# A token-major mixer residual, modulation sums over a feature-major weight copy, and rope tables from the start of the program

## The chip, the cores and the metric

The kernel runs on one core of a Trainium2 chip. The metric is the device time of one execution in microseconds (us); lower is better. The engines are TensorE (PE, its weight loads as PEld), VectorE (DVE), ScalarE (ACT), GpSimd (POOL) and SyncE (SP), whose queue here only issues DMAs.

## The reference

One decoder block over 256 tokens of width 2048, in float32: six modulation vectors from a conditioning vector, a mixer of gated linear attention (GLA) and latent attention (MLA) with a merged output, a SwiGLU FFN and a last RMSNorm. Cut to what matters here:

```python
ang = positions.astype(jnp.float32)[..., None] * inv_freq      # rope, 32 frequencies
cos, sin = jnp.cos(ang), jnp.sin(ang)
mod = (silu(c) @ ada_w + ada_b).reshape(B, 6, D)
shift_m, scale_m, gate_m, shift_f, scale_f, gate_f = mod       # m = 0 .. 5
h = rmsnorm(x, norm_mix_g) * (1 + scale_m) + shift_m
x = x + gate_m * token_mix(h, cos, sin, w_in, ..., w_out)      # ends with merged @ w_out
h = rmsnorm(x, norm_ffn_g) * (1 + scale_f) + shift_f
x = x + gate_f * swiglu(h, ffn_w_in, ffn_w_down)
return rmsnorm(x, final_norm_g)
```

## The kernel before

All weights (408 MB with the modulation weights) come once from memory. A weight tile, 128 partitions x 1024 elements of float32 (512 KB, "a half"), is loaded by SP (`load_raw`, L98), split by an ACT cast into a high part `hi` (L107) and by VectorE into the rest `lo` (L108), and used in three matmuls per tile: hi x hi, lo x hi, hi x lo. `form_a` (L166 to L168) holds the activations still and streams 512 weight columns, and gives token-major results; `form_b` (L176 to L178) holds the weights and streams 256 tokens, and gives feature-major ones (features on the partitions). So a form_b step has twice the matmuls of half the columns.

The stages in order: a start that loads x, turns it feature-major and modulates the first two of 16 feature blocks; the input projection in four rounds r = 0 to 3 over growing parts of the features, so that it can begin before all of the modulation is there; attention of both kinds; the output projections mla_wo and gla_wo; w_out; the FFN's two halves; the final norm.

The modulation is background work. `ada_steps(m, c0)` loads 512 columns of `ada_w` in eight loads; each is scaled by silu(c) and added up on VectorE (L265, L267), two passes of 128x512 per load. The sum over the 128 partitions is then made by four TensorE transposes (L289) whose copies on ACT add up (L291). m = 0, 1 are used by `modulate` (L320 to L322), which makes the FFN's or mixer's input from normed x; m = 2 is the mixer's gate, m = 3, 4 are the FFN's, m = 5 the FFN's gate, which has a POOL all-reduce (L300) in place of the transposes. `pace` sets how many background steps go beside each half; `background(n)` does n steps at once. In `w_out` `background(1000)` ahead of column 3 clears what is left. Where `hold` is set, or with `keep_in_program_order`, an instruction keeps its place in its engine's row; the others are placed by a scheduler when the program is built, and each engine then goes through its row in order.

Load buffers go round: six `raw` tiles, and four more cut from a free slot (`more_raw`; slot 5 in the output projections), so ten there. A load waits until its buffer has been read.

w_out is done in four columns i = 0 to 3 of 512 features by `form_b`. Its results are multiplied by the gate and added to x in feature-major form (L846); x comes back from a copy in DRAM, `x_sp`, written in round 3 (L428, L843). Sums of squares for the FFN's norm are made by ACT and TensorE (L853 to L858), then `rsqrt_mean` (L193 to L206), `rows_of` (L212, L213) and 16 `modulate`. In the FFN `turn_x1` (L899) turns the residual token-major again for the end.

The rope angles (`rope_angles`, L351 to L374) are 40 POOL operations over 128 x 256 angles, in rounds 1 and later; the tables are made in round 3.

Of the kernel before, what the change touches and what calls it, by code (L numbers as in the profile page):

```python
# [17 lines left out]
D = 2048  # L18
# [16 lines left out]
def _consts():  # L35
    j = np.arange(P)
    f = np.zeros((P, 256 + 2), np.float32)
# [3 lines left out]
    f[:, 256] = inv[j % 32]  # L41
    f[:, 257] = np.where(j < 64, 1.0, -1.0)
# [9 lines left out]
def tile_block(ctx: ExitStack, tc: tile.TileContext, x, positions, ada_w, ada_b, w_in, gla_gk_w, gla_wo,  # L52
# [138 lines left out]
    def rsqrt_mean(dst, ssq, n, w, eng=None):  # L191
# [3 lines left out]
        V.tensor_scalar(out=yi, in0=v.bitcast(I32), scalar1=1, scalar2=None, op0=ALU.logical_shift_right)  # L195
        V.tensor_scalar(out=yi, in0=yi, scalar1=-1.0, scalar2=float(0x5F3759DF), op0=ALU.mult, op1=ALU.add)
# [25 lines left out]
    cft = const.tile([P, 258], F32, name="cft")  # L222
# [5 lines left out]
    nc.gpsimd.dma_start(out=cft, in_=cf)  # L228
# [14 lines left out]
    def ada_steps(m, c0, cols=512, quick=None):  # L243
        kk = 1024 // cols
        accs = [sb(512, t, 2 if t == "ada" else 1)[:, :cols]
                for t in (("ada",) if quick is None else ("ada", "w2" if m else "w3"))]
        b0, nb = m * 16 + c0 // P, cols // P
        cs = slice(b0, b0 + nb)
        ps = None if quick is None else aux_bank()
        n = 0  # L250
        for k0 in range(0, KT, kk):
            raw = load_raw(ada_w[0, k0 * P:(k0 + kk) * P, m * D + c0:m * D + c0 + cols], kk, cols)

            def add(k0=k0, raw=raw):
# [758 lines left out]
```

## Time and profile before

| what | value |
|---|---|
| three runs, median | 1746.09 us (1744.71 to 1747.65) |
| profiled execution, device time | 1749.17 us |
| its span in the trace | 1747.1 us |
| mean granted TensorE clock | 0.987 |
| TensorE / VectorE / ACT / POOL busy | 98% / 70% / 49% / 6% |
| HBM read | 408.51 MB, 239 GB/s over the span |

The device time contains some 2 us outside the span. Terms are reckoned on the span and carried to the median. A matmul's busy time overlaps the next one's, so distances between starts, or a count over a full stretch, tell what one costs.

### The profile page before, as it was taken

What the parts mean: (1) busy time and instruction counts of PE and PEld (TensorE: products, weight loads), DVE (VectorE), ACT (ScalarE), POOL (GpSimd) and SP (SyncE); (2) the same over time, 40 slices, a digit from 0 to 9 for tenths busy, and PEclk for the clock granted to TensorE, in tenths of its full rate; (3) what the DMA queues carried; (4) which work ended last, traced back from release to release, by engine and by line L of the source; (5) the groups of instructions that cost most, each with busy time, mean ns of one, the idle gap of its engine ahead of it and who ended that gap; (6) DMA issues with size and microseconds to landing.
All of it is one profiled execution on the core that took longest, in us unless ns stands there. A gap on an engine that the chain in (4) does not pass through costs nothing. (4 is left out here: it accounts for less than half of the span.)

```text
span 1747.1 us, 24089 instructions
## 1 busy us (share of the span) xinstructions
PE 1705.2 (98%) x8888; PEld 1461.1 (84%) x8888; DVE 1226.6 (70%) x1764; ACT 847.6 (49%) x1300; POOL 99.7 (6%) x136
## 2 busy tenths in 40 slices
PE   6999999999999999999999899999999999999997
PEld 5898899889999887788899888888888888788885
DVE  6899987587787477988887856666664444555556
ACT  4644445355766655544444444444444444444443
POOL 1370000000000001000000000000000000000001
PEclk8999999999999999999999899999999999999998
DMA  9999897655455498999998678778776666555652
GB/s 353 323 325 314 300 302 226 182 188 170 144 151 180 123 313 259 343 372 349 336 323 297 212 206 272 242 232 277 240 232 191 182 191 190 178 189 191 192 191 99
DMA packets 207349, 418.47 MB, mean 240 GB/s; under 512 B 12960, under 2 KB 31840, under 8 KB 206592
## 3 DMA queue, kind: packets, MB, share of 16 engines
q1 hardware_dynamic: 205472, 410.39, 72.1%
q0 software_dynamic: 1616, 6.49, 1.0%
q8 instruction: 69, 1.13, 0.3%
q14 instruction: 48, 0.39, 0.1%
q10 hardware_dynamic: 144, 0.07, 0.0%
HBM read 408.51 MB, written 8.39 MB: 239 GB/s over the span
## 5 line engine op out<-in xcount | busy, mean ns | idle before, releaser
L108 DVE TENSOR_TENSOR lo<-raw,hi 128x1024 fp32r<-128x1024 f32 (+3 forms) x524 | 600.9, 1152 | 396.9 <-ACT hi L107 394.4
L107 ACT CAST hi<-raw 128x1024 fp32r<-128x1024 f32 (+3 forms) x524 | 512.4, 984 | 620.6 <-PE mm L168 391.1
L167 PE MATMUL mm<-lo,s 128*128 128x512 f32 (+1 forms) x1520 | 598.4, 394 | 2.6 <-DVE lo L108 2.6
L168 PE MATMUL mm<-hi,s 128*128 128x512 f32 (+1 forms) x1520 | 590.4, 390 | 1.7 <-DVE s L322 1.7
L166 PE MATMUL mm<-hi,s 128*128 128x512 f32 (+1 forms) x1520 | 543.2, 393 | 4.3 <-ACT hi L107 2.1
L166 PEld LDWEIGHTS mm<-hi,s 128*128 128x128 f32 x1520 | 286.7, 190 | 63.3 <-ACT s L321 3.1
L167 PEld LDWEIGHTS mm<-lo,s 128*128 128x128 f32 x1520 | 287.8, 189 | 61.4 <-DVE lo L108 5.2
L168 PEld LDWEIGHTS mm<-hi,s 128*128 128x128 f32 x1520 | 287.3, 189 | 58.7 <-DVE s L322 2.0
L267 DVE SCALAR_TENSOR_TENSOR ada<-raw,cact,ada 128x512 f32<-128x512 f32 (+1 forms) x293 | 211.1, 724 | 10.5 <-DMA raw<-in_ada_w_dram 7.6
L176 PE MATMUL mm<-s,hi 128*128 128x256 f32 x672 | 191.7, 286 | 0.0
L177 PE MATMUL mm<-s,hi 128*128 128x256 f32 x672 | 190.1, 284 | 0.0
L178 PE MATMUL mm<-s,lo 128*128 128x256 f32 x672 | 188.3, 284 | 0.0
L107 ACT CAST hi<-s 128x1024 fp32r<-128x1024 f32 (+1 forms) x76 | 78.2, 1029 | 106.5 <-PE mm L168 46.2
L176 PEld LDWEIGHTS mm<-s,hi 128*128 128x128 f32 x672 | 128.7, 192 | 0.8 <-issue 0.3
L177 PEld LDWEIGHTS mm<-s,hi 128*128 128x128 f32 x672 | 128.8, 192 | 0.4
L178 PEld LDWEIGHTS mm<-s,lo 128*128 128x128 f32 x672 | 127.5, 192 | 0.0
L108 DVE TENSOR_TENSOR lo<-s,hi 128x1024 fp32r<-128x1024 f32 (+1 forms) x76 | 91.7, 1207 | 27.1 <-ACT hi L107 26.5
L926 PE MATMUL mm<-lo,w 128*128 128x512 f32 x160 | 62.7, 392 | 0.0
L927 PE MATMUL mm<-hi,w 128*128 128x512 f32 x160 | 62.4, 392 | 0.0
L267 DVE SCALAR_TENSOR_TENSOR ada<-s,cact,ada 128x512 f32<-128x512 f32 (+1 forms) x79 | 57.7, 730 | 0.5
L925 PE MATMUL mm<-hi,w 128*128 128x512 f32 x160 | 50.5, 394 | 0.7 <-ACT w L933 0.7
L451 DVE TENSOR_TENSOR s<-mm,s 128x512 f32<-128x512 f32 (+1 forms) x62 | 40.1, 672 | 0.2
(270 smaller groups left out, 1594.1 us busy)
## 6 DMA issues: line engine op xcount, KB each, us to landing
raw<-in_ffn_w_in_dram SPq DMA_DIRECT2D x176, 512.0 KB, 4.4
raw<-in_ada_w_dram SPq DMA_DIRECT2D x150, 512.0 KB, 4.9
raw<-in_w_in_dram SPq DMA_DIRECT2D x128, 512.0 KB, 4.7
raw<-in_ffn_w_down_dram SPq DMA_DIRECT2D x88, 512.0 KB, 4.4
s<-in_ada_w_dram SPq DMA_DIRECT2D x42, 512.0 KB, 5.9
s<-in_w_in_dram SPq DMA_DIRECT2D x32, 512.0 KB, 4.7
raw<-in_mla_wo_dram SPq DMA_DIRECT2D x20, 512.0 KB, 6.5
raw<-in_gla_wo_dram SPq DMA_DIRECT2D x20, 512.0 KB, 6.9
```

Of the source, the lines that this page charges most:

```text
L107: A.copy(out=hh_, in_=rr)
L108: V.tensor_tensor(out=ll_, in0=rr, in1=hh_.bitcast(F32), op=ALU.subtract)
L166: T.matmul(ps[t][:, :cols], lhsT=ah[:, k, ts], rhs=hi, start=st, stop=False)
L167: T.matmul(ps[t][:, :cols], lhsT=ah[:, k, ts], rhs=lo, start=False, stop=False)
L168: T.matmul(ps[t][:, :cols], lhsT=al[:, k, ts], rhs=hi, start=False, stop=en)
L176: T.matmul(o, lhsT=hi[:, pick], rhs=ah[:, k], start=st, stop=False, skip_group_check=True)
L177: T.matmul(o, lhsT=hi[:, pick], rhs=al[:, k], start=False, stop=False, skip_group_check=True)
L178: T.matmul(o, lhsT=lo[:, pick], rhs=ah[:, k], start=False, stop=en, skip_group_check=True)
L267: ins = V.scalar_tensor_tensor(out=acc, in0=raw[:, k - k0], scalar=c, in1=acc, op0=ALU.mult, op1=ALU.add)
L925: T.matmul(o, lhsT=ah[:, ts], rhs=hi[:, ns], start=first, stop=False)
L926: T.matmul(o, lhsT=ah[:, ts], rhs=lo[:, ns], start=False, stop=False)
L927: T.matmul(o, lhsT=al[:, ts], rhs=hi[:, ns], start=False, stop=last)
```

## The change

1. m = 0, 1. A transposed copy `ada_t` of the first 4096 columns of `ada_w` is a new input. `ada_cols(k)` computes shift and scale of one block of 128 features: four loads of 128 features x 1024 inputs, each multiplied by a row copy `crow` of silu(c) and summed along the row by one VectorE `tensor_tensor_reduce` (L256). `modulate` of this block follows at once. `crow` is built at the start by four VectorE operations, four matmuls with ones (L414) and four ACT copies.
2. m = 2, 3, 4. The sum over partitions is a POOL `partition_all_reduce` (L294, 12 of them); for m = 3, 4 VectorE then takes the diagonal of four 128x128 blocks (L301), for m = 2 the row goes to DRAM `gm_sp` (L297) and comes back broadcast (L863). Each of these 12 groups has one `yield` more, a background step without a load. The four groups of m = 2 now come first.
3. w_out uses `form_a`; x1 is token-major, x is read again from the input (L866), gate and addition are two VectorE operations per token half (L888, L889), ACT squares with a sum. In column 3 the last two halves are kept, so that token half 0 is done first. Ahead of the FFN x1 is turned feature-major by 32 transposes (L905); `turn_x1` is gone.
4. The rope angles are 64 columns wide, made by POOL at the start; `rope_tables` (L384 to L395) copies and transposes them. Its call stands in round 3 of the program text, without pinning.
5. `rsqrt_mean` has one operation less, and at the start runs on VectorE. Small buffers are arranged anew; rounds 0 to 2 have nine load buffers, before eight.

```diff
+    def ada_cols(k, now=False):
+        for m in (1, 0):
+            c = m * 16 + k
+            part = sb(1, "md", 4)
+            for hf in range(2):
+                raw = raw_tile()
+                nc.sync.dma_start(out=raw, in_=ada_t[m * D + k * P:m * D + (k + 1) * P, hf * 1024:(hf + 1) * 1024])
+
+                def dot(raw=raw, hf=hf, c=c, part=part):
+                    V.tensor_tensor_reduce(out=raw, in0=raw, in1=crow[:, hf * 1024:(hf + 1) * 1024], scale=1.0,
+                                           scalar=part if hf else cb[:, c:c + 1], op0=ALU.mult, op1=ALU.add,
+                                           accum_out=mod[:, c:c + 1] if hf else part)
...
+        modulate(k, xTk, rx, 0, hhk, hlk)
...
-        elif m < 5:
-            ps = aux_bank()
-            for i in range(nb):
-                T.transpose(out=ps[:, i * P:(i + 1) * P], in_=acc[:, i * P:(i + 1) * P], identity=ident)
-            for i in range(nb):
-                A.activation(out=acc[:, i * P:(i + 1) * P], in_=ps[:, i * P:(i + 1) * P], func=AF.Copy,
-                             accum_out=mod[:, b0 + i:b0 + i + 1])
+        if m in (2, 3, 4):
+            ar = sb(512, "ada", 2)
+            G.partition_all_reduce(ar, acc, channels=P, reduce_op=bass_isa.ReduceOp.add)
+            yield
+            if m == 2:
+                tc.keep_in_program_order(nc.sync.dma_start(out=gm_sp[:, c0:c0 + cols], in_=ar[0:1]))
+                return
             for i in range(nb):
+                d = ar[:, i * P:(i + 1) * P]
+                V.tensor_tensor_reduce(out=d, in0=d, in1=ident, scale=1.0, scalar=0.0, op0=ALU.mult, op1=ALU.add,
+                                       accum_out=mod[:, b0 + i:b0 + i + 1])
...
+    def rope_tables(ang, ang2):
+        four = sb(512, "sc", 2)
+        V.scalar_tensor_tensor(out=ang2, in0=ang, scalar=-1.0, in1=ang, op0=ALU.mult, op1=ALU.max)
+        V.tensor_scalar(out=ang2, in0=ang2, scalar1=-1.0, scalar2=float(np.float32(np.pi / 2)), op0=ALU.mult,
+                        op1=ALU.add)
+        ps = aux_bank()
+        for i, a in enumerate((ang, ang2)):
+            A.copy(out=four[:, i * S:(i + 1) * S].rearrange("p (t r f) -> p t r f", t=2, r=4),
+                   in_=a.rearrange("p (t f) -> p t f", t=2).unsqueeze(2).broadcast_to([P, 2, 4, 32]))
+            for t in range(2):
+                c = slice(i * S + t * P, i * S + (t + 1) * P)
+                T.transpose(out=ps[:, c], in_=four[:, c], identity=ident)
+        A.activation(out=sin_t, in_=ps[:, 0:S], func=AF.Sin, scale=sgn)
+        A.activation(out=cos_t, in_=ps[:, S:2 * S], func=AF.Sin)
...
+    bg += [ada_steps(2, 512 * b) for b in range(4)]
     for b in range(4):
-        bg += [ada_steps(m, 512 * b) for m in (2, 4, 3)]
+        bg += [ada_steps(m, 512 * b) for m in (4, 3)]
...
     for i in range(4):
         if i == 3:
             background(1000)
-        for n, ps in enumerate(group(form_b, w_out, 512 * i, k256(mh), k256(ml), KT)):
+        ps = [mm_bank(), mm_bank()]
+        cs = slice(512 * i, 512 * (i + 1))
+        kept = []
+        for n in range(KT // 2):
+            w = half(w_out, 2 * n, 512 * i, 512)
+            if i == 3 and n >= 6:
+                kept.append((2 * n, w))
+            else:
+                form_a(ps, w, k256(mh), k256(ml), 2 * n, n == 0, n == 7, 512)
             tick()
...
-            V.scalar_tensor_tensor(out=x1k[:, k], in0=ps[j // 2][:, (j % 2) * S:(j % 2 + 1) * S],
-                                   scalar=mod[:, 32 + k:33 + k], in1=x1k[:, k], op0=ALU.mult, op1=ALU.add)
...
+        for t in range(2):
+            for k, w in kept:
+                form_a(ps, w, k256(mh), k256(ml), k, False, k == KT - 2, 512, (t,))
+            u = sb(512, "sc", 2)
+            j = 2 * i + t
+            V.tensor_tensor(out=u, in0=ps[t], in1=gm[:, cs], op=ALU.mult)
+            V.tensor_tensor(out=x1v[:, t, cs], in0=x1v[:, t, cs], in1=u, op=ALU.add)
+            A.activation(out=u, in_=x1v[:, t, cs], func=AF.Square, accum_out=sq[:, j:j + 1])
...
+                T.transpose(out=ps[:, kk * S + t * P:kk * S + (t + 1) * P],
+                            in_=x1v[:, t, (k + kk) * P:(k + kk + 1) * P], identity=ident)
+        A.copy(out=x1T[:, k * S:(k + 2) * S], in_=ps)
```

The built order of each engine's instructions shows what a scheduler made of this. SP's queue ahead of column 3 of w_out, before (s_6858 is slot 5, four load buffers):

```order
L98 DMA raw<-in_w_out_dram 128x2x512
L98 DMA s_6858<-in_w_out_dram 128x2x512
L98 DMA s_6858<-in_ada_w_dram 128x2x512 x2
L98 DMA raw<-in_ada_w_dram 128x2x512 x3
L98 DMA raw<-in_w_out_dram 128x2x512 x3
L98 DMA s_6858<-in_w_out_dram 128x2x512 x2
L843 DMA s_8370<-x_sp 128x1024
L98 DMA raw<-in_w_out_dram 128x2x512
```

and after (s_6675 is slot 5, sc the broadcast row of the gate):

```order
L102 DMA s_6675<-in_ada_w_dram 128x2x512
L102 DMA raw<-in_ada_w_dram 128x2x512
L863 DMA sc<-gm_sp 128x512
L102 DMA raw<-in_ada_w_dram 128x2x512 x3
L102 DMA s_6675<-in_ada_w_dram 128x2x512
L102 DMA raw<-in_ada_w_dram 128x2x512
L102 DMA s_6675<-in_ada_w_dram 128x2x512 x2
L102 DMA raw<-in_ada_w_dram 128x2x512
L102 DMA s_6675<-in_ada_w_dram 128x2x512
L102 DMA raw<-in_ada_w_dram 128x2x512 x5
L102 DMA s_6675<-in_w_out_dram 128x2x512 x2
```

Before, five ada loads stand ahead of the column's first half; after, sixteen, and slot 5's four buffers are used by ada loads just ahead of column 3's first four halves.

VectorE's row at the same place, before (L846 is the end of column 2):

```order
L267 SCALAR_TENSOR_TENSOR ada<-s_6858,cact,ada 128x512 x2
L108 TENSOR_TENSOR lo<-raw,hi 128x1024 x2
L846 SCALAR_TENSOR_TENSOR s_8370<-mm,mod,s_8370 128x256 x4
L267 SCALAR_TENSOR_TENSOR ada<-s_6858,cact,ada 128x512
L108 TENSOR_TENSOR lo<-raw,hi 128x1024
L855 TENSOR_TENSOR w_9464<-w_9464,e 128x256
L267 SCALAR_TENSOR_TENSOR ada<-s_6858,cact,ada 128x512
L855 TENSOR_TENSOR w_9464<-w_9464,e 128x256
L108 TENSOR_TENSOR lo<-s_6858,hi 128x1024
L267 SCALAR_TENSOR_TENSOR ada<-s_6858,cact,ada 128x512
```

and after (L888, L889, L892 are the end of column 2; mm are TensorE's results):

```order
L888 TENSOR_TENSOR sc<-mm,s_8141 128x512 x2
L889 TENSOR_TENSOR s_8140<-s_8140,sc 128x512 x2
L892 TENSOR_TENSOR sq<-sq 128x2
L284 SCALAR_TENSOR_TENSOR ada<-raw,cact,ada 128x512 x10
L284 SCALAR_TENSOR_TENSOR ada<-s_6675,cact,ada 128x512 x4
L112 TENSOR_TENSOR lo<-s_6675,hi 128x1024
L301 ISA ada,mod<-ada,ident 128x128
L301 ISA mod 128x1
```

Before, casts `lo` of column 3 stand one or two places from L846, with single passes L267 between them. After, fourteen passes L284 stand between the end of column 2 and the first `lo`, then the four reductions L301, a second `lo`, and more passes.

TensorE's row at the start, before (s_87, s_88 are the modulated input; w_210 and ada the partial sums):

```order
L259 MATMUL aux<-cact,raw 128x1 x8
L283 MATMUL aux<-ones,ada 128x1
L283 MATMUL aux<-ones,w_210 128x1
L283 MATMUL aux<-ones,ada 128x1
L283 MATMUL aux<-ones,w_210 128x1
L166 MATMUL mm<-hi,s_87 128x512 x2
L167 MATMUL mm<-lo,s_87 128x512
L168 MATMUL mm<-hi,s_88 128x512
```

and after (s_99 is scratch, sc the copied angles, s_88, s_89 the modulated input):

```order
L414 MATMUL mm<-s_99,ones 128x512 x4
L340 MATMUL aux<-ident,s_93 128x128 x32
L216 MATMUL aux<-e,ones 128x256
L393 MATMUL aux<-ident,sc 128x128 x2
L170 MATMUL mm<-hi,s_88 128x512 x2
L393 MATMUL aux<-ident,sc 128x128 x2
L171 MATMUL mm<-lo,s_88 128x512
L172 MATMUL mm<-hi,s_89 128x512
```

and ACT's row at the start, after (the cast `hi` of a weight is L111; s_85 holds the angles):

```order
L219 COPY s_85<-aux 128x256
L322 ACTIVATE s_88<-e,mod 128x256 x2
L389 COPY sc<-s_85 128x256
L111 CAST hi<-raw 128x1024
L389 COPY sc<-s_85 128x256
L394 ACTIVATE sin_t<-aux,s_85 128x256
L395 ACTIVATE cos_t<-aux 128x256
L111 CAST hi<-raw 128x1024
```

The two pairs of transposes of the angles (L393), and the ACT copies L389 that feed them, stand at and ahead of the first matmuls and casts of the input projection.

## Rows read from the trace of the kernel before

**Rows 1.** Busy time of the engines, from the page

```profile
PE 1705.2 (98%) x8888; PEld 1461.1 (84%) x8888; DVE 1226.6 (70%) x1764; ACT 847.6 (49%) x1300; POOL 99.7 (6%) x136
```

**Rows 2.** Table by stages: busy us (x) of each engine, PEclk, DMA share, GB/s

```profile
0.00:28.00 28.00, 14.07 (x67) 12.13 (x67) 14.73 (x43) 12.40 (x19) 6.58 (x22) 0.85 0.98 362
...
75.00:91.00 16.00, 11.89 (x57) 10.66 (x55) 16.00 (x23) 8.46 (x18) 14.90 (x15) 0.89 0.82 252
...
733.00:822.00 89.00, 88.71 (x397) 73.08 (x396) 77.90 (x96) 41.25 (x61) 0.00 (x0) 1.00 0.98 359
...
910.00:985.00 75.00, 75.00 (x629) 75.00 (x627) 61.05 (x86) 33.31 (x60) 1.15 (x2) 1.00 0.85 290
```

**Rows 3.** Timeline of TensorE in the FFN (start us, us, engine, line, operation)

```profile
1098.55 0.63 PE L166 MATMUL mm<-hi,s 128*128 128x512 f32 x2
1099.01 0.38 PE L899 MATMUL aux<-ident,s 128*128 128x128 f32 x2
...
1099.46 0.39 PE L168 MATMUL mm<-hi,s 128*128 128x512 f32 x1
```

**Rows 4.** Groups by form, 914.7 to 960.8 (columns 1 and 2 of w_out)

```profile
L176 PE MATMUL mm<-s,hi 128*128 128x256 f32 x128 | 36.3, 284 | 0.0
```

**Rows 5.** Timeline of VectorE and POOL, 76 to 83

```profile
76.75 1.45 DVE L108 TENSOR_TENSOR lo<-raw,hi 128x736 fp32r<-128x736 f32 x1
...
77.50 1.40 POOL L356 TENSOR_SCALAR s<-s 128x256 f32<-128x256 f32 x1
...
82.71 0.91 DVE L108 TENSOR_TENSOR lo<-raw,hi 128x736 fp32r<-128x736 f32 x1
```

**Rows 6.** VectorE's groups by form, whole run (busy us, mean ns)

```profile
L108 DVE TENSOR_TENSOR lo<-raw,hi 128x1024 fp32r<-128x1024 f32 x459 | 566.4, 1235 | 387.0 <-ACT hi L107 384.4 <-DMA raw<-in_w_in_dram 0.4
L267 DVE SCALAR_TENSOR_TENSOR ada<-raw,cact,ada 128x512 f32<-128x512 f32 x258 | 194.9, 757 | 10.5 <-DMA raw<-in_ada_w_dram 7.6
...
L827 DVE TENSOR_TENSOR s<-mm,s 128x512 f32<-128x512 f32 x8 | 5.1, 682 | 0.0
...
L564 DVE CUSTOM_DVE_ANT_0 sc<-aux,cft 128x128 f32<-128x128 f32 x16 | 4.6, 287 | 11.4 <-PE aux L560 11.4
```

**Rows 7.** Timeline of the start: first weight cast, first steady matmul

```profile
26.91 1.03 ACT L107 CAST hi<-raw 128x1024 fp32r<-128x1024 f32 x1
...
30.55 0.80 PE L167 MATMUL mm<-lo,s 128*128 128x512 f32 x1 [1.34 <-DVE lo L108]
```

**Rows 8.** DMA issues and timeline of POOL and VectorE, 0 to 30

```profile
cft<-in_cf_dram POOLq DMA_DIRECT2D x1, 129.0 KB, 6.6
...
15.30 0.32 POOL L200 TENSOR_TENSOR rl<-rl,rv 128x2 f32<-128x2 f32 x1
15.49 0.48 DVE L267 SCALAR_TENSOR_TENSOR ada<-raw,cact,ada 128x256 f32<-128x256 f32 x1
...
15.71 0.31 POOL L201 TENSOR_SCALAR rl<-rl 128x2 f32<-128x2 f32 x1
...
16.89 0.19 POOL L200 TENSOR_TENSOR rl<-rl,rv 128x2 f32<-128x2 f32 x1
```

**Rows 9.** Timeline of SP's queue in w_out's column 2

```profile
948.69 3.25 SPq L98 DMA_DIRECT2D raw<-in_w_out_dram  x3
```

**Rows 10.** DMA issues, from the page (KB each, us to landing)

```profile
raw<-in_ffn_w_in_dram SPq DMA_DIRECT2D x176, 512.0 KB, 4.4
```

**Rows 11.** Timeline from w_out's last matmul to the FFN's first

```profile
984.46 0.28 PE L178 MATMUL mm<-s,lo 128*128 128x256 f32 x1
...
987.65 0.16 DVE L193 TENSOR_SCALAR rv<-aux 128x2 f32<-128x2 f32 x1 [0.65 <-PE aux L858]
...
993.01 0.79 PE L166 MATMUL mm<-hi,s 128*128 128x512 f32 x1 [1.18 <-ACT s L321]
```

**Rows 12.** Line 300, POOL's all-reduce: ns min/median/max, first and last start

```profile
L300 POOL PARTITION_ALL_REDUCE w<-ada x4: 3233/3690/4195, 1080.0 to 1282.5; - x4
L300 POOLq MODIFY_POOL_CONFIG  x2: 33/35/37, 976.6 to 976.6; - x2
```

More of the change, by code (lines that the diff above doesn't have):

```diff
@@ L90, in raw_tile, with more_raw, wide @@
         return more[i - RAW] if i >= RAW else slab.tile([P, 1024], F32, name="raw", tag="raw", bufs=RAW)
-    def more_raw(t=None, c0=0, n=4):
-        more[:] = [t[:, c0 + 1024 * i:c0 + 1024 * (i + 1)] for i in range(n)] if t is not None else []
+    def more_raw(*spans):
+        more[:] = [t[:, c:c + 1024] for t, c0, n in spans for c in range(c0, c0 + 1024 * n, 1024)]
         turn[0] -= turn[0] % (RAW + len(more))
+    def wide(dt=F32):
+        t = sb(2048, "w", 1, dt)
+        return [t[:, 512 * i:512 * (i + 1)] for i in range(4)]
     def load_raw(src, kk, cols):
@@ L158, in tick, with form_a @@
             l.step()
-    def form_a(ps, w, ah, al, k0, first, last, cols):
+    def form_a(ps, w, ah, al, k0, first, last, cols, rows=(0, 1)):
         for kk, (hi, lo) in enumerate(w):
             k = k0 + kk
-            for t in range(2):
+            for t in rows:
                 ts = slice(t * P, (t + 1) * P)
@@ L375, in rope_angles @@
         return ang, ra
+    def rope_tables(ang, ang2):
[12 more added lines that the diff above has]
+        A.activation(out=cos_t, in_=ps[:, S:2 * S], func=AF.Sin)
     latv = qk = vtv = None
     gst = slot(6)
-    def ada_pair(c0, cols):
-        yield from both(ada_steps(1, c0, cols), ada_steps(0, c0, cols))
-        for k in range(c0 // P, (c0 + cols) // P):
-            modulate(k, xTk, rx, 0, hhk, hlk)
     gates = [(O_GB, i) for i in range(4)] + [(O_GA, i) for i in range(4)]
@@ L421, in tile_block @@
     bounds = (0, 2, 6, 10, 16)
-    pairs = [[ada_pair(256, 512)], [ada_pair(768, 512)], [ada_pair(1280, 512), ada_pair(1792, 256)], []]
+    pairs = [[ada_cols(k) for k in ks] for ks in (range(2, 6), range(6, 10), range(10, 16), ())]
     bg += [g for p in pairs for g in p]
-    more_raw(scr, 1792, 2)
+    wr = sb(2048, "w")
+    more_raw((scr, 3072, 1), (wr, 0, 2))
     background(2)
@@ L857, in tile_block @@
+    assert not ATT.busy()
+    rc2 = sb(2, "rx")
+    rsqrt_mean(rc2, sq[:, 6:8], D, 2)
+    x1T = slot(0)
+    x1k = k256(x1T)
+    for k in range(0, KT, 2):
+        ps = aux_bank()
+        for kk in range(2):
             for t in range(2):
-                T.matmul(ps[:, t:t + 1], lhsT=(acc if k == KT - 5 else q)[:, t * P:(t + 1) * P], rhs=ones[:, 0:1],
-                         start=k == KT - 5 and t == 0, stop=k == KT - 1, skip_group_check=True)
-    rc2 = sb(2, "rx")
-    rsqrt_mean(rc2, ps[:, 0:2], D, 2)
+                T.transpose(out=ps[:, kk * S + t * P:kk * S + (t + 1) * P],
+                            in_=x1v[:, t, (k + kk) * P:(k + kk + 1) * P], identity=ident)
+        A.copy(out=x1T[:, k * S:(k + 2) * S], in_=ps)
```

190 lines of the change are left out of this document (85 added, 105 removed).

## The prediction, made before the run

> **What bounds the kernel now.** I read the page first: TensorE is busy 1705.2 of 1747.1 us, VectorE 1226.6 [rows 1]. Then a table by stages: in the w_out stage (910 to 985) TensorE is busy in 75.00 of 75 us at full clock, VectorE in 61.05, the DMA engines at 0.85; TensorE loses time at the start (0 to 28) and at the change from round r = 0 to r = 1 (75 to 91) [rows 2], and for 8 us between w_out and the FFN [rows 11]. So nearly everywhere a saved matmul row pays in full and a saved VectorE row pays nothing, as long as weights and their casts stay ahead. Last I read queues and timelines for how far ahead they are, since the change moves loads.
>
> **Gains on TensorE.** All 76 transposes of L289 go. Two transposes put into a stream of L166 to L168 take L168 from 1098.55 + 3 x 0.23 = 1099.24, where it would have been, to 1099.46: 0.11 us each [rows 3]. 76 x 0.11 = -8.4. The 32 of L899 leave the FFN, where nothing hides them: -3.5. Of the 32 of L905, which replace them, 16 stand in w_out's columns 1 and 2 by the order (+1.8), the others in the gap before the FFN (below). A column group of w_out has 192 matmuls of 256 columns before, two groups in 46.1 us, 23.05 each; 96 of 512 columns cost 96 x 0.23 = 22.1 [rows 3, 4]. Three groups: -2.9, with the +1.8 together -1.1; the fourth is below. The four small transposes of L393 add 0.4.
>
> **Change of round, 75 to 91.** TensorE is idle 4.1 of these 16 us and works on at a mean clock of 0.89 (16 x 0.11 = 1.8 more): 5.9 lost, with VectorE at 16.00 of 16 [rows 2]. The casts of 736 columns take 0.91 there in the better cases and 1.45 next to a POOL rope operation [rows 5], and the four `modulate` of an `ada_pair` come in a bunch. After, POOL's rope work lies at the start and each feature block is modulated when its own sums are there; VectorE's work on m = 0, 1 stays about as large (64 reductions over 1024 columns, nearest row the 1.235 of L108, against 128 passes of 0.757 [rows 6]). I take -4.5, between -1 (a saturated VectorE stays) and -6 (all goes).
>
> **The start.** Before, the first weight cast begins at 26.91 and takes 1.03, the steady stream with L167 at 30.55 [rows 7]. After, the first job's weights are the 14th 512 KB load and not the 13th, at the 362 GB/s of this stretch 1.4 us more [rows 2]: +1.4 at least. But the order also puts `rope_tables` ahead of the first job: ACT's L389 ahead of the first cast, L393 ahead of the first L170 on TensorE, L384 on VectorE ahead of the first `lo`. All wait for POOL's angle chain: a third POOL-issued transfer, which lands near 10 us (the first took 6.6 from its issue [rows 8]; with three issues ahead of the chain I put the third's at 3), then 40 operations of 64 columns. Of this size the trace has none. POOL's 2-column operations take 0.32 us and start 0.41 apart, one between two VectorE passes, while VectorE runs, and 0.19 when it doesn't [rows 8]; a 256-column one takes 1.40 beside VectorE's 1.45 [rows 5]. So POOL seems to get one turn per VectorE operation, and reductions of 1.2 us would hold it longer than passes of 0.48 did. Bounds for the end of the chain: 40 operations of 0.33 (0.19, and as an estimate 0.14 for the other 62 columns and the gap) end at 23, which costs nothing beyond the +1.4; or POOL gets 13 turns of 1.3 us until VectorE itself stops at L384 (27), then 27 x 0.33: 36. I take 32, nearer to the second since VectorE has 8 reductions queued by then. From there L384 (0.2), L389 (0.4), the cast (1.03) and `lo` (1.24): the stream starts at 35, **+4.5** (+1.4 to +8.5). [...]
>
> **Column 3 of w_out.** This is the largest term. Each of the 12 groups of m = 2, 3, 4 now has one background step that issues no load, at unchanged paces, so more work is left for `background(1000)` ahead of column 3. By the order, SP issues 5 ada loads in a row there before, and 16 after. Before, that cost nothing: column 3's first half was issued at 948.69 [rows 9], while column 2 ran until 984.58 - 23.05 = 961.5 [rows 11]. After, VectorE has queued behind L888, which waits for TensorE's last matmul of column 2 (time T), 14 passes L284 in one block and only then the first `lo` of column 3; and since ten buffers go round, the first half can only be issued when the 7th of the 16 ada loads is used up. Working: four epilogue operations of 0.68 and one of 0.16, 2.9; 14 x 0.757 = 10.6, so the block ends at T + 13.5, the 7th load is used at T + 12.0. Issue to landing 4.4 and the cast 1.03: TensorE begins again at **T + 17.5** [rows 6, 7, 10]. Then the second wait: `lo` until 18.7, four L301 behind POOL's all-reduce (3.69 from 13.5 [rows 12]; 4 x 0.37 as an estimate, the custom operation of 0.287 [rows 6] and a short read), second `lo`, L864, the 9th load's two passes: T + 23.7. Only then is the third half issued: cast by T + 29.2. From there each half needs 1.23 + 2 x 0.757 = 2.7 on VectorE and 2.7 on TensorE; column 3 ends near T + 47, before at T + 23.05. Behind it VectorE waits for the last all-reduce (last pass about 42, + 3.7), four L301, three `lo` of the FFN and four epilogue operations stand in its row: T + 54; square and its read 0.8 (an estimate: half a cast of 1024 columns and a read), then the same rsqrt and modulate path, 5.4 from L193 (987.65) to the FFN's first matmul (993.01) [rows 11]: T + 60.5, the transposes of L905 within it. Before it was 993.01 - 961.5 = 31.5. So **+29**. A cruder check: from T to its last `lo` VectorE has about 39 us of work (29 passes, 8 `lo`, 8 L301, the rest), against TensorE's 22 in column 3.
>
> **Other waits.** In the stages before w_out, L301 stands two casts (2.5 us) behind its all-reduce of 3.69: VectorE loses some 1.2 us and 1.5 for the four, 6 times; there it is busy 77.90 of 89 us [rows 2], so most hides: +2 (0 to +5). SP waits as long at the four writes L297 (0 to +1 each, hidden as long as loads are a buffer ahead). The square root one operation shorter, the removed x_sp copy and the removed row sums lie beside other work: nothing.
>
> **Sum.** -8.4 - 3.5 - 1.1 + 0.4 - 4.5 + 4.5 + 29 + 2 = +18.4. The profiled execution has a span of 1747.1 and a time of 1749.2; the median of the runs is 1746.1. 1746.1 + 18.4 = 1764.5; I say **1764**.
>
> **Rivals.** A, the gains win. If column 3's first halves come ahead after all (a buffer other than I read), L284's block still holds back the first `lo`: start at T + 14.7, column 3 over at T + 36.8, the gap as before: +13.7. With the start at +1.4, the round at -6 and no other wait: 13.7 + 1.4 - 6 - 12.6 = -3.5, 1742, just faster. For it: the profile has hidden such loads before [rows 9]. Against: the block stands in one in-order queue. It decides if column 3 costs under 14.
> B, one stall but not the second: +16.5 in place of 29 and the rest as in the forecast: +6, 1752; with A's start and round 1747, no change.
> C, POOL as the new bound. It goes back and forth between plain operations and all-reduce three times by the order, and its angle chain holds the start. At +8.5 for the start, +5 for the waits and a second stall as reckoned: +25.4, 1771.5. If a switch of its code costs anything, more. In the trace the configuration (976.6) lies over 100 us ahead of the first all-reduce (1080.0) [rows 12], so a price can't be seen. [...]
>
> **How the numbers follow.** Forecast 0.56 (1757 to 1769), A 0.17, B 0.10 (0.07 of it within 0.2%, the rest slower), C 0.17. A measurement of this kernel can't tell under 0.2% (3.5 us) from no change. Faster 0.17, same 0.07, slower 0.76. The range takes in forecast, B, most of C and the upper edge of A: 1742 to 1777.
>
> **What would show it.** Right: a TensorE gap of 13 us or more at the end of column 2, ended by a cast, with VectorE full of L284; a second gap of about 8 us some 5 us later; SP's first w_out load of column 3 issued after T; first L170 stream at 33 to 37 behind L389; the stalls at 75 to 91 gone; no gain in the FFN but L899's. Wrong: column 3 without a gap (then the order did not bind), or a start at 30 (then POOL was quick), or gaps at L301 in the output projections as long as POOL's 3.7.

## The result

The changed kernel takes 1769.97 us (median of four runs, 1769.46 to 1771.32), the kernel before 1746.28 in the same comparison: ratio 1.0136, 95% interval 1.0123 to 1.0149. The change makes the block 23.7 us slower; 1764 was forecast, with 1742 to 1777 as the range.

The two traces are laid side by side by the matmuls that open each stage (starts in us):

| place | before | after | gained or lost in the stage that ends here |
|---|---|---|---|
| steady stream of the input projection (third matmul) | 30.55 | 39.88 | +9.3 |
| its 204th matmul (round 0 but for its last three jobs) | 69.05 | 77.22 | -1.2 |
| its 504th matmul (round 1's feature-major jobs done) | 118.75 | 119.17 | -7.8 |
| output gates, first matmul | 606.71 | 604.29 | -2.8 |
| mla_wo, first matmul | 705.94 | 702.25 | -1.3 |
| gla_wo, last matmul | 890.03 | 884.93 | -1.4 |
| w_out, column 2, last matmul | 960.99 | 952.99 | -2.9 |
| w_out, column 3, last matmul | 984.46 | 1006.36 | +29.9 |
| FFN, first matmul | 993.01 | 1017.63 | +2.7 |
| FFN, last matmul of its first half | 1488.27 | 1507.19 | -5.7 |
| end | 1747.12 | 1768.12 | +2.1 |

So up to column 2 of w_out the new kernel is 8.0 us ahead; column 3 and the gap behind it lose 32.6; the FFN gives 3.6 back. Together that is 21.0 and not 23.7: the profiled execution of the kernel before took 1749.17 us, 2.9 more than its median here, that of the changed kernel 1769.90, as its median. The table by stages answers [rows 2] (columns as there):

```profile
0.00:28.00 28.00, 12.54 (x42) 7.34 (x42) 16.23 (x40) 13.46 (x22) 17.99 (x30) 0.81 0.95 349
...
75.00:91.00 16.00, 16.00 (x103) 16.00 (x103) 14.02 (x23) 8.32 (x14) 1.68 (x1) 1.00 0.96 321
...
733.00:822.00 89.00, 89.00 (x394) 73.44 (x393) 81.40 (x108) 38.31 (x37) 9.87 (x3) 1.00 1.00 360
...
910.00:985.00 75.00, 54.83 (x237) 43.67 (x236) 58.64 (x88) 23.42 (x34) 6.47 (x2) 0.85 0.75 252
```

From 75 to 91 TensorE is now busy in 16.00 of 16 us at full clock, before 11.89 at 0.89. From 910 to 985 it is busy in 54.83 of 75, at a clock of 0.85, where before it had all 75.

The place itself, in the timeline of all engines (start, us, engine, line, operation, in brackets the idle time before it and what ended it; SPq is SP's queue):

```profile
952.99 0.39 PE L172 MATMUL mm<-hi,s 128*128 128x512 f32 x1
...
956.18 7.83 DVE L284 SCALAR_TENSOR_TENSOR ada<-raw,cact,ada 128x512 f32<-128x512 f32 x10
...
964.05 3.12 DVE L284 SCALAR_TENSOR_TENSOR ada<-s,cact,ada 128x512 f32<-128x512 f32 x4
965.62 1.94 SPq L102 DMA_DIRECT2D s<-in_w_out_dram  x2
...
971.10 1.04 ACT L111 CAST hi<-s 128x1024 fp32r<-128x1024 f32 x1 [14.07 <-DMA s<-in_w_out_dram]
...
972.20 1.22 PE L170 MATMUL mm<-hi,s 128*128 128x512 f32 x2 [15.96 <-ACT hi L111]
...
974.48 0.63 PE L171 MATMUL mm<-lo,s 128*128 128x512 f32 x1
...
974.90 0.63 PE L172 MATMUL mm<-hi,s 128*128 128x512 f32 x1
...
977.47 1.94 SPq L102 DMA_DIRECT2D s<-in_w_out_dram  x2
...
982.34 0.74 PE L170 MATMUL mm<-hi,s 128*128 128x512 f32 x2 [2.07 <-ACT hi L111]
...
987.82 0.74 POOL L916 DMA_DIRECT2D s<-in_ada_b_dram  x1 [17.25 <-DVE lo L112]
...
997.49 1.04 ACT L111 CAST hi<-raw 128x1024 fp32r<-128x1024 f32 x1 [6.75 <-DMA raw<-in_w_out_dram]
```

The last matmul of column 2 begins at 952.99. VectorE then does fourteen passes L284 until 967.2; SP issues column 3's first half only at 965.62, when the seventh ada load is used up; it is cast at 971.10, and TensorE begins at 972.20 after 15.96 us of waiting for that cast. The third half is issued at 977.47, and TensorE waits for its cast again, 2.07 us. ACT stands another 6.75 us for the seventh half, cast at 997.49. From 987.82 two loads of 1 MB each that POOL issues (L916, L917, the FFN's gate and the last norm's gain, into slot 5, which the column had just left) share the DMA engines with it; by queue, from 986 to 1000 (packets, MB, share of 16 engines; q0 is POOL's):

```profile
q1 hardware_dynamic: 1291, 2.49, 48.8%
q0 software_dynamic: 288, 2.10, 40.3%
```

That they are why it was late is likely, but no run took them away.

### The profile page after: what moved, and what is told of

It reads as the page before. It is cut to its first block, busy times and chain, and to the rows that moved or that the text cites. A ratio compares the mean times of both kernels' runs of the same rounds, so it can differ in the third digit from the quotient of the medians.

```text
span 1768.1 us, 23022 instructions
## 1 busy us (share of the span) xinstructions
PE 1694.1 (96%) x8388; PEld 1427.0 (81%) x8388; DVE 1235.1 (70%) x1797; ACT 832.2 (47%) x1154; POOL 121.2 (7%) x139
## 4 chain that ended last, share of the span: by engine, by line
PE 90%; DVE 4%; POOL 2%; issue 2%; DMA 1%; ACT 1%; DVEq 0%; ACTq 0%; POOLq 0%
PE mm L171 20%; PE mm L172 20%; PE mm L170 20%; PE mm L180 3%; PE mm L181 3%; PE mm L182 3%; PE mm L959 2%; PE mm L960 2%; PE mm L961 2%; PE gx L685 2%; PE gx L960 1%; PE aux L960 1%; PE aux L959 1%; PE gx L959 1%; PE aux L961 1%
## 5 line engine op out<-in xcount | busy, mean ns | idle before, releaser
L111 ACT CAST hi<-raw 128x1024 fp32r<-128x1024 f32 (+3 forms) x518 | 506.5, 984 | 567.6 <-PE mm L172 400.1
L171 PE MATMUL mm<-lo,s 128*128 128x512 f32 (+1 forms) x1648 | 647.1, 393 | 2.4 <-DVE lo L112 2.2
L172 PE MATMUL mm<-hi,s 128*128 128x512 f32 (+1 forms) x1648 | 640.9, 390 | 0.0
L170 PE MATMUL mm<-hi,s 128*128 128x512 f32 (+1 forms) x1648 | 587.1, 392 | 22.8 <-ACT hi L111 21.6
L170 PEld LDWEIGHTS mm<-hi,s 128*128 128x128 f32 x1648 | 310.3, 189 | 88.7 <-ACT hi L111 24.3
L171 PEld LDWEIGHTS mm<-lo,s 128*128 128x128 f32 x1648 | 311.8, 189 | 67.5 <-DVE lo L112 6.0
L172 PEld LDWEIGHTS mm<-hi,s 128*128 128x128 f32 x1648 | 311.7, 189 | 61.6 <-issue 0.7
L284 DVE SCALAR_TENSOR_TENSOR ada<-raw,cact,ada 128x512 f32<-128x512 f32 x191 | 143.0, 749 | 15.4 <-DMA raw<-in_ada_w_dram 12.8
L111 ACT CAST hi<-s 128x1024 fp32r<-128x1024 f32 (+1 forms) x65 | 67.5, 1039 | 114.5 <-PE mm L172 66.6
L180 PE MATMUL mm<-s,hi 128*128 128x256 f32 x416 | 118.5, 287 | 0.0
L181 PE MATMUL mm<-s,hi 128*128 128x256 f32 x416 | 117.4, 284 | 0.0
L182 PE MATMUL mm<-s,lo 128*128 128x256 f32 x416 | 115.4, 285 | 0.0
L180 PEld LDWEIGHTS mm<-s,hi 128*128 128x128 f32 x416 | 79.6, 191 | 0.8 <-issue 0.3
L181 PEld LDWEIGHTS mm<-s,hi 128*128 128x128 f32 x416 | 79.6, 191 | 0.4
L182 PEld LDWEIGHTS mm<-s,lo 128*128 128x128 f32 x416 | 78.3, 191 | 0.0
L294 POOL PARTITION_ALL_REDUCE ada<-ada x12 | 45.2, 3763 | 269.5 <-DVE ada L284 269.5
```

The source lines that it names most:

```text
L111: A.copy(out=hh_, in_=rr)
L170: T.matmul(ps[t][:, :cols], lhsT=ah[:, k, ts], rhs=hi, start=st, stop=False)
L171: T.matmul(ps[t][:, :cols], lhsT=ah[:, k, ts], rhs=lo, start=False, stop=False)
L172: T.matmul(ps[t][:, :cols], lhsT=al[:, k, ts], rhs=hi, start=False, stop=en)
L180: T.matmul(o, lhsT=hi[:, pick], rhs=ah[:, k], start=st, stop=False, skip_group_check=True)
L181: T.matmul(o, lhsT=hi[:, pick], rhs=al[:, k], start=False, stop=False, skip_group_check=True)
```

## Experiments

The theory was that two parts of the change cost time, each by the order in which the engines are fed: the work left over ahead of column 3, and the wait for POOL's angles at the start; and that everything else gains what TensorE no longer has to do. The first four runs take these apart.

**Paces in the attention stage.** In the changed kernel (the attention stage and the output gates):

```diff
-    pace[0] = 0.2
+    pace[0] = 0.3
...
-    pace[0] = 0.6
+    pace[0] = 0.75
```

> The changed kernel with the pace of the background raised in the attention stage (0.2 to 0.3) and in the output-gate stage (0.6 to 0.75); by the order some five ada loads are left ahead of column 3 of w_out in place of sixteen. Backlog theory: from the end of column 2 to the FFN's first matmul, 64 us in the changed kernel, falls to about 33, nothing else moves, 1738 us (1733 to 1745), faster than the kernel before. Rival, work only moved: VectorE is fuller in the attention stage and TensorE waits there for what it no longer waits for in column 3: over 1755.

Measured: 1747.76 us (1744.30 to 1748.35), against the kernel before 1.0008 (0.9998 to 1.0017). From the last matmul of column 2 (957.74) to the FFN's first (992.93) it is 35.2 us in place of 64.6: 29 us of the backlog's price are gone. But 5 us came back elsewhere: mla_wo, which lasts 92.9 us in the changed kernel, lasts 96.6 here, and column 2 ends 4.8 us later. The theory of the backlog holds, but 22 us come back in the end and not the 32 that were expected: the rival has a part.

**Paces in the output projections** of the changed kernel (mla_wo, gla_wo):

```diff
-    pace[0] = 0.8
+    pace[0] = 0.9
...
-    pace[0] = 0.65
+    pace[0] = 0.83
```

> The changed kernel with the pace raised in the output projections only (mla_wo 0.8 to 0.9, gla_wo 0.65 to 0.83); about five ada loads are left ahead of column 3. Backlog theory as for the other pace: about 1738. Rival, transfers as the bound: the DMA share in mla_wo is 1.00 already, so eight loads more in the two stages, 1.4 us each, show there as TensorE waits: about 1749.

Measured: 1755.70 us (1754.67 to 1757.85), 1.0063 (1.0048 to 1.0078): 14 us come back where the theory had 32. Column 2 ends 6.5 us later than in the changed kernel (959.45 against 952.99): mla_wo and gla_wo, at DMA shares of 0.99 and 0.95, are 3.2 and 2.8 us longer. That is the rival's part. From mla_wo to the FFN TensorE waits for casts and low parts (columns: who waits for whom, us in total, times, longest):

```profile
PE mm L170 <- ACT hi L111: 6.1, 3, 2.7
PE mm L171 <- DVE lo L112: 5.4, 8, 1.5
```

But the larger part of what is missing lies in column 3 itself, which neither theory had: from column 2 to the FFN it still takes 42.4 us (959.45 to 1001.89), with the other pace 35.2, though five loads stand in a row ahead of the column in both. Here seven passes come in a row on VectorE, and TensorE waits for a cast behind them:

```profile
967.08 1.53 DVE L284 SCALAR_TENSOR_TENSOR ada<-s,cact,ada 128x512 f32<-128x512 f32 x2
...
968.65 3.90 DVE L284 SCALAR_TENSOR_TENSOR ada<-raw,cact,ada 128x512 f32<-128x512 f32 x5
...
973.71 0.73 PE L170 MATMUL mm<-hi,s 128*128 128x512 f32 x2 [2.67 <-ACT hi L111]
```

So the number of loads left over does not give the price by itself; the order that is built of them has a part.

**The kernel before, with a backlog.** Nothing of the change, only lower paces in the output projections, so that 15 ada loads are left ahead of column 3:

```diff
-    pace[0] = 0.8
+    pace[0] = 0.62
...
-    pace[0] = 0.65
+    pace[0] = 0.5
```

> The kernel before with lower paces in the output projections (0.8 to 0.62, 0.65 to 0.5), nothing else: fifteen ada loads in a row are left ahead of column 3 of w_out, and a block of some sixteen passes stands ahead of its first low-part cast on VectorE. Backlog theory: a TensorE gap of 14 us or more at the end of column 2 and 20 to 30 us more in all, 1766 to 1776. Rival, the cost needs the new parts (all-reduce, reductions behind it, the longer epilogue): under 10 us, below 1756.

Measured: 1771.67 us (1770.29 to 1773.82), 1.0154 (1.0139 to 1.0169): 25.9 us slower, as much as the whole change. The timeline shows the same picture without any new part:

```profile
966.38 7.84 DVE L267 SCALAR_TENSOR_TENSOR ada<-raw,cact,ada 128x512 f32<-128x512 f32 x10
...
972.67 8.05 SPq L98 DMA_DIRECT2D raw<-in_w_out_dram  x3
...
974.27 1.12 PE L289 MATMUL aux<-ident,ada 128*128 128x128 f32 x4 [13.44 <-DVE ada L267]
978.02 1.04 ACT L107 CAST hi<-raw 128x1024 fp32r<-128x1024 f32 x1 [15.41 <-DMA raw<-in_w_out_dram]
...
979.12 0.58 PE L176 MATMUL mm<-s,hi 128*128 128x256 f32 x1 [3.73 <-ACT hi L107]
```

Ten passes in a row, SP's first half of column 3 behind them, and TensorE idle for 13.44 and 3.73 us. From column 2 to the FFN it takes 57.9 us (960.11 to 1017.97), in the kernel before 32.0, in the changed one 64.6. So the amount of background work ahead of column 3 is the cause; the all-reduce, the reductions behind it and the token-major epilogue can have a part in the last 6.8 us only (there with sixteen loads, here with fifteen).

**Rope tables late.** In the changed kernel the VectorE operation and the two ACT copies of `rope_tables` keep their place in round 3:

```diff
-        V.scalar_tensor_tensor(out=ang2, in0=ang, scalar=-1.0, in1=ang, op0=ALU.mult, op1=ALU.max)
+        pin(V.scalar_tensor_tensor(out=ang2, in0=ang, scalar=-1.0, in1=ang, op0=ALU.mult, op1=ALU.max))
...
-            A.copy(out=four[...], in_=a...)
+            pin(A.copy(out=four[...], in_=a...))
```

> The changed kernel with the rope tables pinned to the place in round 3 where their call stands; POOL's angle chain stays at the start, nobody waits for it there. Start theory: the first stream of matmuls begins at 31 to 33 in place of 39.9 and all of it is kept: 1762. Rival, weights as the bound: rounds 0 and 1 run at the pace of the transfers (share 0.99 in the kernel before), the late start lets loads pile up and gives time back, so round 1 ends at most 2 us sooner: 1768 to 1770.

Measured: 1765.47 us (1763.19 to 1765.55), 1.0113 (1.0097 to 1.0130): 4.5 us less than the changed kernel, between the two. The stream starts at 33.45 in place of 39.88:

```profile
30.72 1.22 PE L170 MATMUL mm<-hi,s 128*128 128x512 f32 x2 [4.38 <-ACT hi L111]
33.45 0.80 PE L171 MATMUL mm<-lo,s 128*128 128x512 f32 x1 [1.50 <-DVE lo L112]
```

Of these 6.4 us, 6.6 are kept at the 504th matmul (112.56 against 119.17) and 6.5 at mla_wo's first matmul (695.74 against 702.25), so the rounds are not held by the transfers, and the rival falls. 2.5 are lost in mla_wo, where TensorE waits 2.2 us for one cast, at 711.63; ACT stood 8.21 us ahead of it for the load of that weight. Why it landed late stays open.

**One buffer against four.** The wide buffer of the changed kernel is cut into four tiles again; rounds 0 to 2 lose two load buffers with it:

```diff
-        t = sb(2048, "w", 1, dt)
-        return [t[:, 512 * i:512 * (i + 1)] for i in range(4)]
+        return [sb(512, t, 1, dt) for t in ("w2", "w3", "w0", "w1")]
...
-    wr = sb(2048, "w")
-    more_raw((scr, 3072, 1), (wr, 0, 2))
+    more_raw((scr, 3072, 1))
```

> The changed kernel with the one wide buffer of 2048 columns cut into four tiles of 512 again, in the order of the kernel before; rounds 0 to 2 lose two of their nine load buffers with it. Placement theory: the matmuls of the FFN's second half, 233 ns apart in the changed kernel and 229 before, come back to 229, and the stretch from the FFN's last L170 to the end shortens from 260.9 to about 257 us. Rival, the spacing has another cause (the residual's place, the order of loads): 261 as in the changed kernel. For rounds 0 and 1: if nine buffers did a part of what the change gains there, they take over 1 us longer; else the same 37.3 and 42.0 us. Time 1766 by the first, 1770 by the rival.

Measured: 1770.48 us (1768.65 to 1772.76), no difference to the changed kernel. The stretch from the last matmul of the FFN's first half to the end (the expectation calls it the last L170) falls from 260.9 to 258.2 us, not far from the 257 of the placement theory, but not by the spacing: from the first to the last of the second half's 1056 matmuls it takes 246.0 us, in the changed kernel 246.3. The 2.6 us come from the seam between the halves, where the order changed. The last matmul of the first half and the first one of the second, in the changed kernel and then in this run:

```profile
1507.19 0.39 PE L172 MATMUL mm<-hi,s 128*128 128x512 f32 x1
...
1510.00 0.50 PE L959 MATMUL mm<-hi,w 128*128 128x512 f32 x1 [0.65 <-ACT w L968]
```

```profile
1512.81 0.40 PE L171 MATMUL mm<-hi,s 128*128 128x512 f32 x1
1513.04 0.40 PE L957 MATMUL mm<-hi,w 128*128 128x512 f32 x1
```

The transposes that stand in that gap in the changed kernel now lie among the second half's matmuls; between neighbours without one it is 0.232 us, against 0.233 and, in the kernel before, 0.230. So the placement theory is not borne out but for a third of the spacing at most. The gain is lost earlier: from the 504th matmul to the output gates it takes 489.8 us in place of 485.1. In rounds 0 and 1 the run says nothing, since the order changed there too (the angles' copies moved behind the first cast).

**The norm of the GLA outputs on VectorE**, in the changed kernel:

```diff
-        rsqrt_mean(r, st, GDV, 2, G)
+        rsqrt_mean(r, st, GDV, 2)
```

With the `G` POOL goes back and forth there between its plain operations and the all-reduce. Line 202 is the first plain operation; its queue has three pairs of rows MODIFY_POOL_CONFIG (first and last start), each a change of configuration, which the expectations call a change of code:

```profile
L202 POOL TENSOR_TENSOR rl<-gr x12: 187/195/707, 609.8 to 716.2; 128x2 f32<-128x2 f32 x12
L202 POOLq MODIFY_POOL_CONFIG  x6: 42/98/98, 602.6 to 680.4; - x6
```

The timeline at the first change, the operand and the operation that waits for it:

```profile
605.61 0.17 DVE L199 TENSOR_SCALAR gr<-rv 128x2 int32<-128x2 int32 x1
...
609.80 0.71 POOL L202 TENSOR_TENSOR rl<-gr 128x2 f32<-128x2 f32 x1 [7.30 <-DVE ada L284]
```

The first change stands at 602.6, the operand is ready at 605.8 (L199), and the operation begins at 609.80, 7.2 us behind the change; the last stands at 680.4, the operation follows at 688.28, 7.9 us behind.

> The changed kernel with the norm of the GLA outputs made by VectorE alone, so that POOL runs nothing but all-reduces from there on and changes its code once. In the changed kernel the first plain POOL operation begins 7 to 8 us after each of two changes although its operand is there 4 us earlier, and VectorE waits 5.5 us for those results. Code theory: the output-gate stage loses TensorE waits of 2 to 4 us: 1767. Rival, the waits lie beside other work: 1770, no change.

Measured: 1768.16 us (1767.71 to 1769.28), 1.8 us less than the changed kernel, whose runs all lie above these; output gates 96.8 us in place of 98.0. That is between theory and rival: the changes cost less than 2 us here.

**Both causes taken away.** Late rope tables as above, and a pace of 0.45 or 0.55 in the attention stage, no other pace changed:

```diff
-    pace[0] = 0.2
+    pace[0] = 0.45
```

> Rope tables pinned late, and a pace of 0.45 in the attention stage alone; two ada loads in a row are left ahead of column 3. If start and backlog are separate costs, their gains add: 1770 - 4.5 - 29 = 1737, below the kernel before. Rival, the attention stage takes no more background for nothing (one run lost 5 us in the stage behind it): 1742 to 1746.

> As the run with 0.45 but 0.55: all of the background is done ahead of column 3, so VectorE waits for no all-reduce there and no reduction stands ahead of the last epilogue. Backlog theory: another 2 to 3 us less between column 2 and the FFN than with 0.45, 1735. Rival, attention as the new bound: its stage grows by more than that, 1742 or more.

Measured: 1745.10 us (1742.65 to 1746.77), 0.9992 (0.9983 to 1.0001), and 1747.08 us (1742.09 to 1750.23), 0.9999 (0.9986 to 1.0011). Both miss: no better than the kernel before. Column 3 is cured in both (31.4 us from column 2 to the FFN), but the stages in front of it became longer: with 0.45 the output gates take 106.8 us, not 98.0. VectorE's waits from 600 to 985 name the reason for 0.45 (who waits for whom, us in total, times, longest):

```profile
DVE ada L282 <- POOL ada L294: 10.4, 1, 10.4
```

POOL's timeline with 0.45 at that place:

```profile
622.67 3.25 POOL L294 PARTITION_ALL_REDUCE ada<-ada  x1 [5.96 <-issue]
```

And the timeline of POOL and VectorE with 0.55:

```profile
732.85 3.25 POOL L294 PARTITION_ALL_REDUCE ada<-ada  x1 [8.11 <-issue]
...
736.13 0.29 DVE L301 CUSTOM_DVE_ANT_0 ada<-ada,ident 128x128 f32<-128x128 f32 x1 [7.58 <-POOL ada L294]
```

A single wait of 10.4 us: L282, the first pass of the next group, needs a buffer that the all-reduce still reads (the expectation quoted below puts this down to L301, which is wrong for that run). The all-reduce began only at 622.67, 5.96 us behind the norm's last operation; the norm's first one began at 611.92, 7.9 us behind its change of configuration at 604.0. In the changed kernel the all-reduce's queue has such rows too (L294, eight, 499.8 to 718.8). With 0.55, POOL's last plain operation ended at 724.7, its all-reduce began at 732.85, and VectorE stood 7.58 us. So POOL's going back and forth, worth 1.8 us in the changed kernel, holds VectorE up when the background runs faster.

**Both causes and the change of configuration.** The two runs again, with the norm on VectorE by the edit shown above:

> The run with late rope tables and pace 0.45, and the norm of the GLA outputs on VectorE, so that POOL does not go back and forth between plain operations and all-reduces. There TensorE stood 7.1 us (621 to 628) behind a reduction L301 whose all-reduce began 5.7 us after POOL's second change of code, after a first plain operation 7.9 us behind its change. Code theory: that stall and some 2 us of smaller ones go, 1745 - 8 = 1737, faster than the kernel before by 0.5%. Rival, the reduction waits for something else (the all-reduce's own 3.2 to 4.7 us): 1742 to 1745.

> The same with pace 0.55. There the stall of 4.7 us at 734 stood behind an all-reduce that began 8.1 us after POOL's last operation, with no wait shown. Code theory: 1747 - 6 = 1741. Rival, attention is too full at this pace whatever POOL does: 1745 or more.

Measured: 1734.97 us (1731.76 to 1736.38), 0.9931 (0.9917 to 0.9945), and 1741.17 us (1739.32 to 1743.40), 0.9968 (0.9955 to 0.9981). The first beats both kernels, by 11 and 35 us. The wait of 10.4 us is gone from VectorE's list and no wait for POOL is left in it:

```profile
DVE lo L112 <- ACT hi L111: 44.2, 44, 3.4
DVE s L819 <- PE mm L172: 1.8, 1, 1.8
DVE e L321 <- PE aux L216: 1.4, 1, 1.4
DVE s L865 <- DMA sc<-gm_sp: 1.2, 1, 1.2
```

With 0.55 TensorE still loses time in the attention stage; the output gates begin at 611.48 against 603.10.

**The price of the transposes.** As the best run, but m = 3, 4 summed by transposes and ACT as in the kernel before, without POOL, without L301, without the extra background step; the pace is 0.3 then:

```diff
-        if m in (2, 3, 4):
+        if m == 2:
...
+        if m in (3, 4):
+            ps = aux_bank()
+            for i in range(nb):
+                T.transpose(out=ps[:, i * P:(i + 1) * P], in_=acc[:, i * P:(i + 1) * P], identity=ident)
```

> As the run with pace 0.45 and the norm on VectorE, but m = 3, 4 summed by TensorE transposes and ACT as in the kernel before (no POOL, no reduction L301, no extra background step for these eight groups; pace 0.3 so that three ada loads are left ahead of column 3). Price of the transposes by the forecast's own row: 32 x 0.11 = 3.5 us on TensorE, so 3 to 4 us above that run if the all-reduce costs nothing beside it. Rival, the waits of VectorE behind POOL cost as much as the transposes: the same time within 2 us, or less.

Measured: 1734.71 us (1733.77 to 1736.76), 0.9932 (0.9920 to 0.9944): the same, as its rival had it. For m = 3, 4 the all-reduce is worth nothing in the total. That VectorE and the queues behind POOL take what TensorE saves is not shown, since the pace differs too: the way from the 504th matmul to the output gates is 4.1 us shorter here (486.9 against 491.0), mla_wo and gla_wo are 4.2 and 2.7 longer.

## Why the prediction was right, point by point

**Right in kind and place.** The term that decided, column 3, was read from the order and priced from rows of before, and each step of the chain can be found in the trace: the block of passes ends at T + 14 (forecast T + 13.5, with T = 953.2 as the end of column 2), the first half is issued at T + 12.4 (12.0), the third at T + 24.3 (23.7), cast at T + 29.1 (29.2). The price was +32.6 and the forecast +29. The run of the kernel before with a backlog shows the cause by itself.

**Sizes that were off in that term.** The first half's way from issue to cast took 5.5 us and not 4.4, so TensorE began at T + 19.0, not 17.5. The second wait was announced as about 8 us (by the sum's own terms, T + 17.5 + 2 x 2.7 to T + 29.2, it is 6.3) and was 2.07. It began 1.5 later, and TensorE took 8.1 us for the first two halves and not 5.4: after the 15.96 us of waiting its granted clock was 0.50 until 976.6, with matmuls 0.43 us apart in place of 0.23. Two more such stretches follow in this column, each some 2 us behind a wait for a cast (2.07 us until 982.34, 2.56 until 998.58; table by stages, TensorE's granted clock in the third column from the end):

```profile
972.20:976.60 4.40, 4.36 (x9) 2.98 (x10) 4.37 (x14) 1.05 (x1) 0.00 (x0) 0.50 0.03 10
984.20:986.80 2.60, 2.60 (x8) 2.02 (x7) 0.52 (x2) 1.05 (x1) 0.00 (x0) 0.50 0.87 310
1000.60:1004.00 3.40, 3.40 (x9) 2.67 (x8) 0.99 (x1) 0.77 (x2) 3.37 (x1) 0.50 1.05 387
```

The step that failed here is "from there each half needs 2.7": column 3 ended at T + 53.4, not T + 47. From the third half's first matmul (982.34) to the column's last (1006.36) it takes 24.0 us, where 71 distances of 0.227 would be 16.1. Of the 7.9 between, 4.1 are waits, 2.7 of them for the late seventh half (the sum had left out the two 1 MB transfers that POOL issues, the likely reason), and 3.7 are the lower clock, which the sum had nowhere. Behind the column it took 11.0 us to the FFN and not 13.5, so the price as a whole was off by less, 3.6.

**The start: mechanism right, size too small.** +4.5 was forecast, +9.3 came, just outside the +1.4 to +8.5 of that term. The rows that answer [rows 8]:

```profile
11.00 0.19 POOL L363 CAST s<-s 128x2 f32<-128x2 int32 x1 [7.08 <-DMA s<-in_positions_dram]
...
16.85 1.28 DVE L256 CUSTOM_DVE_ANT_0 raw<-raw,s,md 128x1024 f32<-128x1024 f32 x1
17.00 1.32 POOL L360 TENSOR_TENSOR s<-s 128x64 f32<-128x64 f32 x1
...
33.12 0.32 POOL L360 TENSOR_TENSOR s<-s 128x64 f32<-128x64 f32 x1
...
36.90 0.24 POOL L379 TENSOR_SCALAR s<-s 128x64 f32<-128x64 f32 x1
37.17 0.41 ACT L389 COPY sc<-s 128x256 f32<-128x256 f32 x1 [9.50 <-POOL s L379]
```

The chain begins at 11.0 and ends at 37.1. The same POOL operation of 64 columns (L360) takes 1.32 us next to a reduction of 1.28, and 0.32 alone. While VectorE does its first eight reductions (12.46 to 23.9), POOL starts ten operations, eight of them 1.0 to 1.5 us long: about one turn per reduction, as was read from [rows 8]. The step that failed is the end of the chain, put at 32 between 23 and 36; the upper bound was the right one and even it a little low, since the third transfer landed near 11 and not 10, and the operations start 0.42 apart when alone and not 0.33.

**The change of round: larger than forecast.** -4.5 was taken, at most -6. From the start of the stream to the 504th matmul the kernel gained 8.9. The 5.9 us of [rows 2] went in full; the eight transposes of L289 in these rounds, booked under another term, add about 1 us, and 1.2 came in round 0 already; the rest, under 1 us, wasn't followed up. Which part of the change did it (the angles' work gone from beside the casts, each block modulated by itself, or the ninth load buffer) no run separates. The errors of the start (+4.8) and of this step (-4.4) nearly cancel: at the 504th matmul the kernel stood at +0.4, forecast 0. That is luck, and the total owes part of its nearness to it.

**TensorE's savings.** From there to the end of gla_wo -5.5, and -2.9 in w_out's columns 0 to 2: -8.4 together, where the forecast had -8.4 - 1.1 + 0.4 + 2 = -7.1 (some of it in the rounds ahead). The FFN's first half gained 5.7 and not 3.5. Of that, 1.3 are the clock at its start: behind the idle time ahead of the FFN the granted clock is 0.50 from 993.0 to 999.2 in the kernel before, and from 1017.6 to 1021.0 in the changed one. If the other 4.4 are all L899's, its transposes cost 0.14 us each, and the price of 0.11, read from one pair, was somewhat low. The second half lost 2.1 that the forecast did not have: its matmuls take 3.4 us more from first to last (rows below), and the end behind them is 1.4 shorter.

**Rivals.** A and B fell: the column has both waits. C's time, 1771.5, is nearer to the measured one than the forecast is, and the band of 1757 to 1769 was missed by 1 us: C's long start (+8.5) came, but its waits of +5 did not, since the stages from the 504th matmul to column 2 gained 1.3 more than forecast. C's price for a switch of POOL could not be seen before. In the changed kernel 7.2 and 7.9 us passed from a change of configuration to the next operation, but the changes were not the bound that C made of POOL there. With paces of 0.45 and 0.55 VectorE stood 10.4 and 7.58 us behind an all-reduce that began 5.96 and 8.11 us after POOL's operation before it. At the start there was no such distance: L365 begins 0.1 us behind its change. The range's upper end, 1777, lies 5.5 above C's sum, and no run shows that a switch of POOL adds so much to this kernel's time: with the norm on VectorE it is 1.8 us less.

## What to carry to other kernels

A step that issues nothing still takes a turn: where a background is spread by counting steps, a step more per group leaves real work over, and it comes out at the one place that waits for all of it. Read that place in the built order of SP and of the casting engine: with fourteen passes ahead of the column's first `lo` TensorE stood 15.96 us, with ten in a row in the kernel before with a backlog 13.44 and 3.73, though VectorE's busy share of the changed kernel's span is 70%, as in the kernel before. Before POOL gets a second kind of work, look at what stands behind each change of kind: here 5.96 to 8.11 us passed before the next operation where a pace was raised. And look at a chain of many small POOL operations beside long VectorE operations: eight of ten took 1.04 to 1.47 us beside reductions of 1.28, where the last ones of the chain, alone, took 0.24 to 0.37.

## What was not expected of the hardware

From a change of POOL's configuration to the norm's operation behind it, 7.2 and 7.9 us passed in the changed kernel, 7.9 with a pace of 0.45 (604.0 to 611.92) and 7.1 with 0.55 (611.0 to 618.1). In the first two the operand was there 4.0 us ahead of the operation. From the norm's last operation to the all-reduce it was 5.96 us with 0.45 and 8.11 with 0.55; there the view names nothing that was waited for (`issue`). At the start of the changed kernel L365 began 0.1 us behind its change; why stays open.

The spacing of 512-column matmuls in the FFN's second half differs between the kernels though the matmuls are the same: 0.230 us before and 0.233 after, 242.84 and 246.27 us from the first to the last of 1056 (before and then after):

```profile
1491.06 0.50 PE L925 MATMUL mm<-hi,w 128*128 128x512 f32 x1 [0.65 <-ACT w L933]
...
1733.90 0.40 PE L927 MATMUL aux<-s,w 128*128 128x512 f32 x1
```

```profile
1510.00 0.50 PE L959 MATMUL mm<-hi,w 128*128 128x512 f32 x1 [0.65 <-ACT w L968]
...
1756.27 0.39 PE L961 MATMUL aux<-s,w 128*128 128x512 f32 x1
```

In the first half the median is 0.227 in both. Cutting the wide buffer left the second half at 246.05 us from first to last; what sets the spacing stays open.
